# Where the query and key projections of a hybrid attention layer run: as jobs between attention steps, or as a stage of their own ahead of the linear attention

## The chip, the cores and the metric

The kernel runs on one core of a Trainium2 chip. The core has a matrix engine (TensorE, "PE" in the profile, its weight loads "PEld"), a vector engine (DVE), an activation engine (ACT), GpSimd (POOL) and SyncE (SP), which here issues the DMAs. Each engine works through its own instructions in order. The metric is the device time of one execution in microseconds (us); fewer is better.

## The reference

One inference step of one layer, for a prompt of 1024 frames and a sample of 32 further frames (together T = 1056 columns), model width 1024, everything in float32:

```python
gq, gk, gv, la, gg, dq, dk, dv, dg, ma, mb = in_proj(rmsnorm(hp, pre_norm_g), w_in, gla_w_a2, gla_b_a)
dq, dk = rope(dq, pos), rope(dk, pos)          # the first 16 of each 64 channels are rotated
o_gla, s_p = gla_prompt(gq, gk, gv, la)        # gated linear attention, 4 heads, chunked
o_diff = diff_prompt(dq, dk, dv, lam)          # 8 heads; two softmax maps m = 0, 1 per head
...
# diff_attend, per head and block of 128 queries:
s = q @ k / 8, masked by chunks of 64;  p = softmax(s)
attn = p[m=0] - lam * p[m=1];  out = attn @ v
...
yg = rmsnorm(o_gla) * silu(gg);  yd = rmsnorm(o_diff) * 0.8 * silu(dg)
merged = sigmoid(ma) * (yg @ w_proj_gla) + sigmoid(mb) * (yd @ w_proj_diff)
y = x + rmsnorm(merged @ w_out)
```

The rotated keys of all heads (`newk`) and the values are outputs too. The sample frames run the same layer against a cache of 512 past keys and values.

## The kernel before, in words

Activations stand as `X`: channels on the 128 partitions, 8 tiles deep, T columns, each split into a high and a low float32r part. A projection of 128 output channels is a **job**: 3 stretches of 352 columns, 8 tiles deep, and 3 matmuls each (high by high, low weights, low activations; L458, L459, L460), so 72 matmuls. `wtile` loads a job's weights (one raw buffer, two buffers for each split part), ACT makes the high part (L426), POOL the low part (L428).

The stages, in order: normalisation and the value projections (to 222 us of the profile); the linear attention ("GLA", 4 heads); the differential attention ("diff", 8 heads, which is the subject here); the output projection of the GLA branch; that of the diff branch (L436 to L438); the last projection and the norm (L1174 to L1196).

Inside the GLA and the diff stage the order on PE is written by a small planner, the class `Order`. Threads yield steps, each with a cost, a list of events that must have happened (with a latency after each) and the PSUM banks that it takes. `run` looks through the threads in their order and takes the first whose step is ready by the planner's own clock; the latencies are the table `W`, in us. The attention thread stands first, the sample thread second and `fill`, which works through the list of jobs in steps of 6 matmuls, last. So a job's matmuls are placed where attention would not yet be ready. The order so found is the order in which PE executes; on the chip it waits for the real semaphores. PE instructions of a later stage may be placed among those of an earlier one, but each stage keeps its own order.

In a diff head (`diff_main`, `diff_scores`) there are 8 query blocks i of 128 queries. For block i and each map m: the scores (L878, L879, width w = 128(i+1)) go to one of two large PSUM banks, DVE masks and takes the maximum (L880, L882), ACT the exponential (L884), and DVE combines the two maps (L887 to L889). Then PE transposes the result in groups of up to 4 blocks into the one bank "t" (L926), ACT and DVE split it (L928, L929), and after each second block the product with the values follows (L939 to L941). The scores of block i+1 are issued ahead of the transposes of block i. The head's end is `diff_fin` (L852 to L861), after the first scores of the next head. The latencies that pace this are `sm`, `sm_w`, `sm_s` (scores to a free bank), `p`, `p_w` (scores to the combined map), `tr_t` (transposes to a free bank: 2.27) and `at` (2.45).

The jobs of the diff stage before are: for each head a query job and a key job (`rot_job`), a job `dgate_job` for the silu gate (it needs `diff_fin` of the head before, and `diff_fin` of its own head needs it), and 12 of the 16 `gate_job`s for the merge gates, which can stand anywhere; `GATES_GLA` and `GATES_DIFF` say how many go with which head. A `rot_job` evacuates PSUM to one tile `rr`, fetches the partner channels of the rotation by four small DMAs, multiplies on POOL (L793) and DVE (L795), adds (L797), and splits into high and low parts (`split_q` L807 to L811, `split_k` L826 to L829, with DMAs that copy the halves of `k` and `kl` to the other 64 partitions). Queries have two buffers, keys one.

Of the kernel before, what the change touches and what calls it, by code (L numbers as in the profile page):

```python
# [11 lines left out]
F32 = mybir.dt.float32  # L12
# [31 lines left out]
GATES_GLA = [0, 1, 1, 1, 1]  # L44
GATES_DIFF = [2, 1, 1, 1, 1, 1, 1, 2, 2]
# [3 lines left out]
N = {"fin": 1, "rr": 3, "q": 2, "k": 4, "fill": 2, "first": 200, "evac": 1200, "lead": 2}  # L49
# [73 lines left out]
def hybrid_step_kernel(ctx: ExitStack, tc: tile.TileContext, a):  # L123
# [54 lines left out]
    ptd = dram.tile([KT, P, T], F32, name="ptd")  # L178

# [300 lines left out]

    gp = pool("gp", reuse_waits="tile")
# [273 lines left out]
    ct = dp.tile([P, T], F32, name="ct")  # L755
    dma(ct, a["ropec"])
    stb = dp.tile([P, T], F32, name="stb")
    dma(stb, a["ropes"])
    sw = dp.tile([P, T], F32, name="sw")
    nc.gpsimd.memset(sw, 0.0)  # L760

    for n, dt, tags in ((T, F32, ("rr",)), (NP, F32R, ("q00", "q10")), (NP, F32, ("p0", "p0", "p1")),
                        (NP, F32R, ("vh", "vl")), (NQ * 256, F32R, ("ah", "al")),
                        (NP, F32R, ("k0", "k1", "kl0", "kl1", "q01", "q11"))):
        for tag in tags:
            dp.tile([P, n], dt, tag=tag, bufs=tags.count(tag), name="first")
# [15 lines left out]
    SC = HD ** -0.5  # L782

    def rot_job(b, event, needs, split):
        def begin():
            r = dp.tile([P, T], F32, tag="rr", name="rr")

            def done():
                for m in range(2):
                    o = m * HD  # L790
                    dma(sw[o : o + 8], r[o + 8 : o + 16])
                    dma(sw[o + 8 : o + 16], r[o : o + 8])
                nc.gpsimd.tensor_tensor(sw, sw, stb, op=ALU.mult)  # L793
                for c in parts(T, N["rr"]):
                    ve.tensor_tensor(r[:, c], r[:, c], ct[:, c], op=ALU.mult)  # L795
                for c in parts(T, N["rr"]):
                    ve.tensor_tensor(r[:, c], r[:, c], sw[:, c], op=ALU.add)  # L797
                split(r)
            return (lambda ps, sl: act(r[:, sl], ps, AF.Copy)), done
        return b, event, begin, needs  # L800

    def split_q(h):
        def f(r):
            q0 = dp.tile([P, NP], F32R, tag=f"q0{h % 2}", name="q0")
            q1 = dp.tile([P, NP], F32R, tag=f"q1{h % 2}", name="q1")
            for c in parts(NP, N["q"]):
                act(q0[0:64, c], r[0:64, c], AF.Copy, scale=SC)  # L807
                act(q1[64:128, c], r[64:128, c], AF.Copy, scale=SC)
                ve.scalar_tensor_tensor(q0[64:128, c], r[0:64, c], SC, q0[0:64, c].bitcast(F32),
                                        op0=ALU.mult, op1=ALU.subtract)  # L810
                ve.scalar_tensor_tensor(q1[0:64, c], r[64:128, c], SC, q1[64:128, c].bitcast(F32),  # L811
                                        op0=ALU.mult, op1=ALU.subtract)
            qsam[h] = sam(0, h)
            act(qsam[h], r[:, NP:T], AF.Copy, scale=SC)
            dqs[h] = q0, q1
        return f

    def split_k(h):
        def f(r):
            st(a["newk"][h], r)  # L820
# [10 lines left out]
            for t, src, dst in ((k0, 0, 64), (k1, 64, 0), (kl0, 0, 64), (kl1, 64, 0)):  # L831
                dma(t[dst : dst + 64].bitcast(F32), t[src : src + 64].bitcast(F32))
# [449 lines left out]
```

## Time and profile before

| | |
|---|---|
| median of 3 runs | 1516.63 us (1512.86 to 1523.22) |
| the profiled execution | 1523.35 us, span 1521.6 us |
| granted PE clock, mean | 0.981 |
| PE busy | 1438.6 us, 95% of the span |
| PEld busy | 1340.6 us, 88% |
| DVE busy | 792.0 us, 52% |
| ACT busy | 623.2 us, 41% |
| POOL busy | 298.4 us, 20% |
| DMA queue of SP | 150.71 MB, 30.9% of 16 engines' span |

A row of a group reads: line, engine, operation, output <- inputs, shapes, count | busy us, mean ns of one | idle time ahead and what ended it. Matmuls overlap in the records: one of 352 columns is recorded with some 320 ns and the next starts 160 ns later, so for PE the distance of starts is the cost. A row of stretches reads: from:to, length, then busy us and count for each engine, the granted PE clock, the DMA share and GB/s.

### The profile page before, as it was taken

What the parts mean: (1) busy time and instruction counts of PE and PEld (TensorE: products, weight loads), DVE (VectorE), ACT (ScalarE), POOL (GpSimd) and SP (SyncE); (2) the same over time, 40 slices, a digit from 0 to 9 for tenths busy, and PEclk for the clock granted to TensorE, in tenths of its full rate; (3) what the DMA queues carried; (4) which work ended last, traced back from release to release, by engine and by line L of the source; (5) the groups of instructions that cost most, each with busy time, mean ns of one, the idle gap of its engine ahead of it and who ended that gap; (6) DMA issues with size and microseconds to landing.
All of it is one profiled execution on the core that took longest, in us unless ns stands there. A gap on an engine that the chain in (4) does not pass through costs nothing.

```text
span 1521.6 us, 22330 instructions
## 1 busy us (share of the span) xinstructions
PE 1438.6 (95%) x8848; PEld 1340.6 (88%) x8848; DVE 792.0 (52%) x1464; ACT 623.2 (41%) x1282; POOL 298.4 (20%) x186
## 2 busy tenths in 40 slices
PE   8999999989999998998999998989899999999997
PEld 6787789889989898998989897989798889999997
DVE  5602005655474343757685866677764544155415
ACT  4603114635353323564655564555555443022311
POOL 1200002222222233121222222212221112122001
PEclk9999999999999999999999998999999999999999
DMA  8621111221222144131323132223212187433305
GB/s 294 205 104 37 44 48 43 61 85 56 89 70 78 58 145 130 46 88 60 102 75 88 60 102 76 74 73 88 89 50 89 67 271 248 168 130 117 109 1 187
DMA packets 66118, 152.29 MB, mean 100 GB/s; under 512 B 9920, under 2 KB 28480, under 8 KB 65488
## 3 DMA queue, kind: packets, MB, share of 16 engines
q1 hardware_dynamic: 66000, 150.71, 30.9%
q8 instruction: 74, 1.21, 0.3%
q14 instruction: 44, 0.36, 0.1%
HBM read 100.16 MB, written 39.98 MB: 92 GB/s over the span
## 4 chain that ended last, share of the span: by engine, by line
PE 51%; DVE 7%; ACT 4%; DMA 2%; issue 1%; POOL 1%; SPq 0%; DVEq 0%; POOLq 0%; ACTq 0%
PE ps_w L458 9%; PE ps_w L459 9%; PE ps_w L460 9%; PE ps_w L437 2%; PE ps_w L436 2%; PE ps_w L438 2%; PE ps_c L1176 2%; PE ps_c L1174 2%; PE ps_c L1175 2%; PE ps_t L926 2%; PE ps_s L879 2%; PE ps_s L878 2%; DVE p L888 1%; DMA kl<-kl 1%; PE po L940 1%
## 5 line engine op out<-in xcount | busy, mean ns | idle before, releaser
L458 PE MATMUL ps_w<-X,wh 128*128 128x352 f32 x1344 | 455.2, 339 | 7.5 <-ACT k L489 3.2
L459 PE MATMUL ps_w<-X,wl 128*128 128x352 f32 x1344 | 440.2, 328 | 0.0
L460 PE MATMUL ps_w<-X,wh 128*128 128x352 f32 x1344 | 438.3, 326 | 0.0
L428 POOL TENSOR_TENSOR wl<-wr,wh 128x1024 fp32r<-128x1024 f32 x72 | 178.5, 2479 | 688.5 <-ACT wh L426 551.2
L458 PEld LDWEIGHTS ps_w<-X,wh 128*128 128x128 f32 x1344 | 257.9, 192 | 12.5 <-DVE sg L471 4.0
L459 PEld LDWEIGHTS ps_w<-X,wl 128*128 128x128 f32 x1344 | 257.9, 192 | 1.2 <-issue 1.2
L460 PEld LDWEIGHTS ps_w<-X,wh 128*128 128x128 f32 x1344 | 258.5, 192 | 0.0
L884 ACT ACTIVATE p<-ps_s,nm 128x256 f32<-128x256 f32 (+7 forms) x128 | 94.4, 740 | 60.8 <-DVE nm L882 35.9
L426 ACT ACTIVATE wh<-wr 128x1024 fp32r<-128x1024 f32 x72 | 75.9, 1054 | 61.0 <-PE ps_w L460 35.7
L283 PE MATMUL ps_v<-wh,X 128*128 128x512 f32 x248 | 97.6, 394 | 1.4 <-DVE X L222 1.4
L282 PE MATMUL ps_v<-wh,X 128*128 128x512 f32 x248 | 98.3, 397 | 0.0
L284 PE MATMUL ps_v<-wl,X 128*128 128x512 f32 x248 | 98.2, 396 | 0.0
L882 DVE TENSOR_REDUCE nm<-ps_s 128x1 f32<-128x256 f32 (+7 forms) x128 | 95.0, 746 | 2.7
L880 DVE MEMSET ps_s<- 64x64 f32 x128 | 14.3, 112 | 118.4 <-PE ps_s L879 116.9
L269 DVE TENSOR_TENSOR vo<-ps_v,vo 32x512 f32<-32x512 f32 x4 | 2.7, 679 | 140.7 <-ACT vo L268 140.7
L926 PE MATMUL ps_t<-ident,p 128*128 128x128 f32 x288 | 49.0, 280 | 25.6 <-DVE ps_s L880 13.8
L928 ACT ACTIVATE ah<-ps_t 128x512 fp32r<-128x512 f32 (+2 forms) x96 | 46.8, 488 | 58.5 <-PE ps_t L926 57.8
L878 PE MATMUL ps_s<-k,q 128*128 128x512 f32 (+2 forms) x192 | 69.3, 368 | 1.2 <-DMA k<-k 1.2
L879 PE MATMUL ps_s<-kl,q 128*128 128x512 f32 (+2 forms) x192 | 65.0, 354 | 4.0 <-DMA kl<-kl 3.8
L643 POOL TENSOR_TENSOR vl<-vr,vh 128x512 fp32r<-128x512 f32 (+1 forms) x20 | 24.8, 1238 | 223.2 <-ACT vh L642 223.2
L265 ACT ACTIVATE vo<-ps_v 128x512 f32<-128x512 f32 x32 | 19.0, 595 | 114.9 <-PE ps_v L284 114.5
L926 PEld LDWEIGHTS ps_t<-ident,p 128*128 128x128 f32 x288 | 35.9, 143 | 32.8 <-issue 22.5
(318 smaller groups left out, 3039.3 us busy)
## 6 DMA issues: line engine op xcount, KB each, us to landing
wr<-w SPq DMA_DIRECT2D x72, 512.0 KB
thd<-gate SPq DMA_DIRECT2D x16, 528.0 KB
xn<-xn SPq DMA_DIRECT2D x16, 512.0 KB
wr<-wv SPq DMA_DIRECT2D x16, 512.0 KB
newk<-rr SPq DMA_DIRECT2D x8, 528.0 KB
ygr<-ygd SPq DMA_DIRECT2D x8, 528.0 KB
tha<-thd SPq DMA_DIRECT2D x8, 528.0 KB
ydr<-ydd SPq DMA_DIRECT2D x8, 528.0 KB
```

The lines of the kernel that those rows point to most:

```text
L282: mm(ps, xk[:, 0, t0 : t0 + P], wh[:, k, :], start=(k == 0), stop=False)
L283: mm(ps, xk[:, 1, t0 : t0 + P], wh[:, k, :], start=False, stop=False)
L284: mm(ps, xk[:, 0, t0 : t0 + P], wl[:, k, :], start=False, stop=(k == KT - 1))
L428: nc.gpsimd.tensor_tensor(wl, wr, wh.bitcast(F32), op=ALU.subtract)
L458: mm(ps[:, :n], wh[:, k, :], src[k][:, 0, t0 : t0 + n], start=(k == 0), stop=False)
L459: mm(ps[:, :n], wl[:, k, :], src[k][:, 0, t0 : t0 + n], start=False, stop=False)
L460: mm(ps[:, :n], wh[:, k, :], src[k][:, 1, t0 : t0 + n], start=False, stop=(k == KT - 1))
L878: mm(ps[:, n0 : n0 + n], qs[m][:, qsl], ks[m][:, n0 : n0 + n], start=True, stop=False)
L879: mm(ps[:, n0 : n0 + n], qs[m][:, qsl], kls[m][:, n0 : n0 + n], start=False, stop=True)
L882: ve.tensor_reduce(nm, ps[:, 0:w], axis=AX.X, op=ALU.max, negate=True)
L884: act(p[:, 0:w], ps[:, 0:w], AF.Exp, bias=nm, accum_out=sm[:, m : m + 1])
L926: nc.tensor.transpose(ps[:, (j - j0) * P : (j - j0 + 1) * P], p[:, j * P : j * P + P], ident)
```

## The change

All 16 query and key projections move out of the diff stage into a stage between the value projections and the GLA stage. They are plain `proj` calls in an order of the scheduler's making, not jobs of the planner. Their results go to DRAM (`qd`, `kd`: 16 half heads of 64 channels by T). After each four heads of keys or of queries, `turn` loads the rotated channels of those four heads into one tile of 128 partitions, its partner channels into another, rotates once and stores them back. In the diff stage `head_load` loads a head's keys and queries from DRAM to both halves of the partitions and splits them; it stands at block 2 of the head before. Keys and queries have two buffers each. The planner's jobs are now 8 + 8 + 2 in the GLA stage (before: 8 + 8 + 4) and 8 + 14 in the diff stage (before: 16 + 8 + 12). The latencies `sm`, `p`, `tr_t`, `at` are as they were.

```diff
-GATES_GLA = [0, 1, 1, 1, 1]
-GATES_DIFF = [2, 1, 1, 1, 1, 1, 1, 2, 2]
+GATES_GLA = [0, 0, 1, 1, 0]
+GATES_DIFF = [2, 2, 2, 2, 2, 1, 1, 1, 1]
-N = {... "q": 2, "k": 4, ...}
+N = {... "q": 2, "k": 2, ...}
-W = {... "dq": 7.76, "dk": 14.32, ...}
+W = {... "dq": 16.0, "dk": 16.0, ...}
...
+    rq = pool("rq", reuse_waits="tile")
+    ct = rq.tile([P, T], F32, name="ct")
+    stb = rq.tile([P, T], F32, name="stb")
...
+    def turn(d, g, new):
+        part = lambda s: d[g * 8 : g * 8 + 8, s * 8 : s * 8 + 8, :]
+        r = rq.tile([P, T], F32, tag="r", name="r")
+        sw = rq.tile([P, T], F32, tag="sw", name="sw")
+        for s in range(2):
+            dma(r[s * HD : s * HD + HD], part(s))
+            dma(sw[s * HD : s * HD + HD], part(1 - s))
+        nc.gpsimd.tensor_tensor(sw, sw, stb, op=ALU.mult)
+        ve.tensor_tensor(r, r, ct, op=ALU.mult)
+        ve.tensor_tensor(r, r, sw, op=ALU.add)
+        for s in range(2):
+            st(part(s), r[s * HD : s * HD + HD])
+            if new is not None:
+                for h in range(4):
+                    o = r[s * HD + h * 16 : s * HD + h * 16 + 16]
+                    st(new[4 * g + h].rearrange("(m d) t -> m d t", m=2)[:, s * 8 : s * 8 + 8, :], o)
+
+    def qk_block(b, d, h, scale, new):
+        r = rq.tile([P, T], F32, tag="nat", bufs=3, name="nat")
+        proj(wtile(b + h), xs, lambda ps, sl: act(r[:, sl], ps, AF.Copy, scale=scale))
+        st(d[2 * h : 2 * h + 2], r)
+        if new is not None:
+            for m in range(2):
+                st(new[h, m * HD + 16 : m * HD + HD, :], r[m * HD + 16 : m * HD + HD])
+
+    for g in range(2):
+        for b, d, scale, new in ((BLK_DK, kd, 1.0, a["newk"]), (BLK_DQ, qd, SC, None)):
+            for h in range(4 * g, 4 * g + 4):
+                qk_block(b, d, h, scale, new)
+            turn(d, g, new)
+    rq.release()
...
-    def rot_job(...), split_q(h), split_k(h)
+    def head_load(h):
+        both = lambda d, m: d[2 * h + m, :, 0:NP].unsqueeze(0).to_broadcast([2, HD, NP])
+        ks, kls, qs = [], [], []
+        for m in range(2):
+            kh = dp.tile([P, NP], F32R, tag=f"k{m}", bufs=2, name=f"k{m}")
+            kl = dp.tile([P, NP], F32R, tag=f"kl{m}", bufs=2, name=f"kl{m}")
+            dma(kl.bitcast(F32), both(kd, m))
+            for c in parts(NP, N["k"]):
+                act(kh[:, c], kl[:, c].bitcast(F32), AF.Copy)
+                ve.tensor_tensor(kl[:, c], kl[:, c].bitcast(F32), kh[:, c].bitcast(F32), op=ALU.subtract)
+            ...
+        for m in range(2):
+            raw = tp.tile([P, NP], F32, tag="sg1", name="qraw")
+            dma(raw, both(qd, m))
+            q = dp.tile([P, NP], F32R, tag=f"q{m}", bufs=2, name=f"q{m}")
+            for c in parts(NP, N["q"]):
+                act(q[:, c], raw[:, c], AF.Copy)
+                ve.tensor_tensor(q[64:128, c], raw[64:128, c], q[64:128, c].bitcast(F32), op=ALU.subtract)
+            qs.append(q)
+        ... # the sample's 32 columns by two small DMAs
+        S.mark(("dq", h))
+        S.mark(("dk", h))
...
         for i in range(NQ):                       # diff_main
+                if i == 2 and h + 1 < DH:
+                    head_load(h + 1)
...
     for h in range(-1, DH):                       # the diff stage's jobs
         n = GATES_DIFF[h + 1]
-            jobs.append(rot_job(BLK_DQ + h + 1, ...))
         jobs += [gate_job(*gates.pop(0)) for _ in range(min(n, 1))]
-            jobs.append(rot_job(BLK_DK + h + 1, ...))
         if h >= 0:
             jobs.append(dgate_job(h))
         jobs += [gate_job(*gates.pop(0)) for _ in range(n - 1)]
+    head_load(0)
```

The matmuls of the kernel are the same in number and shape before and after.

More of the change, by code (lines that the diff above doesn't have):

```diff
@@ L178, in hybrid_step_kernel @@
     ptd = dram.tile([KT, P, T], F32, name="ptd")
+    qd = dram.tile([2 * DH, HD, T], F32, name="qd")
+    kd = dram.tile([2 * DH, HD, T], F32, name="kd")
     def x_pair(name):
@@ L781, in parts @@
         return [slice(i * n // cnt, (i + 1) * n // cnt) for i in range(cnt)]
[L782 to L800, printed above, removed]
```

60 lines of the change are left out of this document (13 added, 47 removed), and 2 rows, old and new, of the table W.

## The prediction

> **What bounds the kernel now.** First the page's busy times and its groups.
>
> ```profile
> PE 1438.6 (95%) x8848; PEld 1340.6 (88%) x8848; DVE 792.0 (52%) x1464; ACT 623.2 (41%) x1282; POOL 298.4 (20%) x186
> L458 PE MATMUL ps_w<-X,wh 128*128 128x352 f32 x1344 | 455.2, 339 | 7.5 <-ACT k L489 3.2 <-DVE sg L471 3.0 <-PEq L572 1.0
> ```
>
> PE is busy nearly all the time, and a job holds 24 of the L458 matmuls, so 1344 are 56 jobs. The change keeps every matmul, so the time can only move by what PE waits. To see where jobs stand I took the busy times by stretch, of L458 alone: the end of the GLA stage, three diff heads (first scores to first scores of the next) and the whole diff stage; then the same stages with all engines, and the projection of the diff branch, which runs as plain `proj` calls.
>
> ```profile
> 558.90:601.79 42.89, 27.71 (x86) 16.13 (x86) 1.00 0.43 129
> 601.79:674.53 72.74, 34.00 (x100) 19.38 (x100) 0.98 0.27 77
> 826.43:901.06 74.63, 32.52 (x96) 18.09 (x96) 1.00 0.29 85
> 1144.22:1220.70 76.48, 29.37 (x84) 16.35 (x84) 0.98 0.24 86
> 601.79:1220.70 618.91, 263.04 (x760) 147.56 (x760) 0.97 0.27 80
> ...
> 601.79:1220.70 618.91, 580.21 (x3628) 546.20 (x3628) 411.67 (x791) 325.97 (x717) 139.54 (x66) 0.97 0.27 80
> 1323.30:1415.50 92.20, 92.20 (x576) 92.20 (x576) 46.88 (x70) 19.19 (x31) 18.42 (x14) 1.00 0.37 123
> ```
>
> The last row gives a job's price: 8 jobs in 92.2 us without a gap, **11.53 us each**. The diff stage takes 618.9 us for 760 / 24 = 31.7 jobs (365 us), so 254 us, 32 us per head, are attention and waits. A head swallows 100, 96 or 84 of L458: 4.2, 4 or 3.5 jobs.
>
> The question that decides is whether the jobs pace a head, or the head's own chain. Head 7 answers: nothing after it needs a query or key job, its jobs ran out before its end, and it still took 76.5 us. So a head is paced by the planner's latencies and the jobs fill them. The same end of a head, transposes of block 7 up to the product with the values, is in the trace once with jobs in between (head 0) and once after the jobs had run out (head 7):
>
> ```profile
> 665.07 0.60 PE L926 MATMUL ps_t<-ident,p 128*128 128x128 f32 x4
> 668.39 0.60 PE L926 MATMUL ps_t<-ident,p 128*128 128x128 f32 x4
> 671.73 0.28 PE L939 MATMUL po<-ah,vh 128*128 128x256 f32 x1
> ...
> 1211.52 0.66 PE L926 MATMUL ps_t<-ident,p 128*128 128x128 f32 x4
> 1213.59 0.66 PE L926 MATMUL ps_t<-ident,p 128*128 128x128 f32 x4 [1.41 <-DVE al L929]
> 1215.92 0.39 PE L939 MATMUL po<-ah,vh 128*128 128x256 f32 x1 [0.36 <-ACT os__13011 L1015]
> ...
> 1218.92 0.27 PE L1024 MATMUL ps_so<-ident,os__13011 64*128 64x64 f32 x1
> ```
>
> Filled, the steps lie 3.32 and 3.34 us apart; bare, 2.07 and 2.33, with PE idle for 1.41; the product's 24 matmuls then take 3.0. A latency without jobs does not vanish: it shrinks to some two thirds, and what is left is PE standing still.
>
> **The change part by part.** *The new stage* has 16 jobs: 16 x 11.53 = **+184.4 us** if it is as dense as the quoted stage of `proj` calls. ACT evacuates as there; `turn`'s work lies beside PE. I add 2 us for its ends (bounds 0 and 40, rival 3). The GLA stage's first head must then wait for the memory of `ct` and `stb`:
>
> ```profile
> 600.54 4.77 DMA kl<-kl
> L793 POOL TENSOR_TENSOR sw<-sw,stb 128x1056 f32<-128x1056 f32 x16 | 40.9, 2554 | 16.2 <-DMA sw<-rr 13.0 <-DVE sg L471 1.9 <-DVE sm L887 1.3
> L795 DVE TENSOR_TENSOR rr<-rr,ct 128x352 f32<-128x352 f32 x42 | 22.0, 543 | 0.0
> L797 DVE TENSOR_TENSOR rr<-rr,sw 128x352 f32<-128x352 f32 x42 | 20.6, 510 | 0.0
> L829 DVE TENSOR_TENSOR kl<-rr,k 64x256 fp32r<-64x256 f32 x28 | 14.0, 501 | 0.8
> L811 DVE SCALAR_TENSOR_TENSOR q<-rr,q 64x512 fp32r<-64x512 f32 x14 | 13.4, 957 | 0.4
> L809 DVE SCALAR_TENSOR_TENSOR q<-rr,q 64x512 fp32r<-64x512 f32 x14 | 13.2, 941 | 1.2 <-ACT q L807 0.8
> L828 DVE TENSOR_TENSOR kl<-rr,k 64x256 fp32r<-64x256 f32 x28 | 11.6, 413 | 0.4
> L1155 DVE TENSOR_TENSOR C<-cwr,C 128x512 fp32r<-128x512 f32 x12 | 7.7, 685 | 6.4 <-ACT C L1154 6.4
> ```
>
> A store, a load (each at most the 4.77 of the DMA row) and POOL's 2.55: some 10 us after the last projection, of which the first two jobs of the stage (23 us) hide all but the planner's early gate steps: I take +4 (0 to 10).
>
> *The GLA stage* gives two gates to the diff stage. The last one counts there. The one after the keys of head 1 filled latencies of head 0; by the two-thirds above its 11.5 us save 6, not 11.5 (0 to 11.5). With the +4 the stage's end moves by **-2**.
>
> *The wait for head 0.* Before, 42.9 us lie between the GLA's last transposes and the first scores, filled by 86 / 24 = 3.6 jobs, two of them the query and key job. Now the loads need only memory; the two query halves pass one after the other through the tile that held the GLA's last gate: twice a DMA (4.77) and a split (three operations, estimated by the 0.685 of the DVE row for a tile of that size), about 13.7 us, with gate jobs beside it. **-30 us** (-43 if the loads come free at once, -20 if they queue on SP behind stores).
>
> *What leaves a head.* The quoted DVE rows L795 to L828 sum to 94.8 us in the diff stage, 12 per head; `head_load` brings 4 x 0.685 for the keys and at most as much for the queries, 5.5 per head. Keys are now loaded a head ahead, so the waits for their copies go:
>
> ```profile
> PE ps_t L926 <- DVE ps_s L880: 13.8, 9, 2.8
> PE ps_t L926 <- DVE sm L887: 5.3, 1, 5.3
> ...
> PE ps_s L879 <- DMA kl<-kl: 3.8, 4, 2.2
> ```
>
> That is 3.8 us in all for the copies, and of the 19 us behind a busy DVE a part. A fully filled head so goes from 77.4 us (618.9 / 8) to about 73.6, between head 0 (72.7) and head 3 (74.6). What is late next is the softmax chain itself, which the change leaves alone. `head_load`'s DMAs wait on SP for the one query tile; behind them stand weights, gate stores and the value load. The weights are a job ahead (11.5 us), so I cost that at nothing; without that cover it is some 5 us per head.
>
> *What is missing in a head.* Fillers: 22 jobs instead of 35.3 (31.7 + 3.6). The job list with the rule that the silu gate of head h waits for the end of head h-1 lets them run so: 1.5 ahead of head 0; 4.2 in head 0; 3.3 in head 1; 3, 3 in heads 2 and 3; 2, 2, 2 in heads 4 to 6; 1 in head 7. The planner is greedy, so the early blocks are filled and the late ones, the longest, stand bare. Head 3, its first stretch up to the scores of block 1, then the whole cut at the scores of blocks 4 and 6 and the transposes of block 7, shows how many of its 96 fall where:
>
> ```profile
> 826.43:832.79 6.36, 3.04 (x8) 1.50 (x8) 1.00 0.42 134
> ...
> 826.43:854.04 27.61, 13.00 (x38) 7.14 (x38) 1.00 0.26 80
> 854.04:868.64 14.60, 6.11 (x18) 3.42 (x18) 1.00 0.22 74
> 868.64:890.14 21.50, 10.00 (x30) 5.65 (x30) 1.00 0.13 31
> 890.14:901.06 10.92, 3.41 (x10) 1.88 (x10) 1.00 0.80 216
> ...
> 879.74 0.44 PE L878 MATMUL ps_s<-k,q 128*128 128x512 f32 x1
> ...
> 881.41 0.39 PE L879 MATMUL ps_s<-kl,q 128*128 128x512 f32 x1
> ...
> 887.50 1.27 DVE L889 SCALAR_TENSOR_TENSOR p<-p,sm 128x1024 f32<-128x1024 f32 x1
> ```
>
> The first 8 fall before the next silu gate is free, so two jobs (48) last to the scores of block 6, three (72) almost to the transposes of block 7, one (24) about to the scores of block 4. Bare, the last piece shrinks by (3.32 + 3.34) - (2.07 + 2.33) = 2.3 us. The third: scores of block 6 (7/8 of those of block 7), transposes and product of block 5 (4.4, and 18 matmuls, 2.2), scores of block 7 (879.7 to 881.8, 2.1 with the first transposes' start), its softmax from 881.8 to 888.8 (7.0): some 17.2 instead of 21.5, so 4.5. The second by the same steps (1.3, 2.3, 1.5, 1.5, 2.1 and 2 for the softmax of block 3) some 10.6 instead of 14.6, so 4. DVE allows no more: it is busy 411.7 / 8 = 51 us per head now and 45 after. Against the filled 73.6: heads 0 and 1 take 72.7 and 72; heads 2 and 3, 70.5 each; heads 4 to 6, 66.8 each; head 7, 62.8. Sum 549; with 5 for the clock (below) 554 instead of 618.9: **-65 us**, for 13.3 jobs (153 us) that left. Bounds: -24 (bare stretches do not shrink) and -181 (rival 1).
>
> *The clock after a wait.* The longest frequent wait and what follows it, and the bare end of head 7:
>
> ```profile
> 1156.70:1160.50 3.80, 1.01 (x7) 0.72 (x6) 3.73 (x5) 0.30 (x1) 2.50 (x1) 1.00 0.61 242
> 1160.50:1165.00 4.50, 4.50 (x20) 4.50 (x20) 2.71 (x7) 1.97 (x6) 0.00 (x0) 0.62 0.49 152
> 1209.00:1221.00 12.00, 8.72 (x63) 6.86 (x61) 3.17 (x9) 6.00 (x14) 2.89 (x2) 1.00 0.59 226
> ```
>
> After 2.8 us idle the granted clock was 0.62 for 4.5 us, 1.7 us lost; through waits of 1.4 us it stayed at 1.00. The bare heads have one long wait each, for the softmax of block 7, and only some will fall so: 5 us. The Trainium skill, "TensorE: Matmul & The Clock Gate", section "Part 1: The HAM clock gate", says that an idle window of about 3.4 us halves the array's clock until it was busy as long again; it speaks against the change. Here a shorter wait sufficed. By the page alone every bare stretch with such a wait would run at half rate, which is rival 4.
>
> **Sum**, against the profiled 1523.35 us: +184.4 + 2 - 2 - 30 - 65 = +89, so 1612. That execution lies 6.7 above the median of 1516.6; against the median the forecast is **1606 us**. With all terms at their ends at once (new stage 184 to 194, GLA -11.5 to +10, start -43 to -20, heads -100 to -45) it would be 1547 or 1656.
>
> **The rivals.** *1, not slower: the bare latencies close up.* If the padding in the planner's latencies is most of them, bare heads fall to the longer of PE's own work (24 us of attention: head 3's 74.6 less 96 x 3 x 0.16 of jobs and less 4.8 idle, the stage's 618.9 - 580.2 over 8; plus its jobs) and DVE's 45: 72.7, 62.5, 58.6 twice, 47 three times, 45, together 438, so -181; with -45 for the start and +184 the time is 1475. It decides below a mean of 58 us per head, where the heads' saving equals the 154 that the other terms cost. For it: DVE is busy only 66% of the stage. Against it: the bare end of head 7, and the 7.0 us softmax. 0.13.
>
> *2, bare stretches don't shrink,* because DVE and the head's loads collide there: heads 74.6, saving 24: 1647. Against it the bare steps of head 7. 0.08.
>
> *3, the new stage is not dense.* `turn`'s loads wait on SP for the stores of the head just projected, and the next job's weights stand behind them; four turns of up to 10 us: 1644. For it: one SP queue issues everything. Against it: the weights' slack of a job. 0.08.
>
> *4, half clock through the bare stretches:* their PE work by the pieces (22 + 7 + 6 us less jobs) is some 70 us over six heads, of which 55 would show in place of the 5: 1656. 0.09.
>
> *The change doesn't do what it says* if the scheduler leaves projections over for later gaps; I see no place for it, since they are ready first. The forecast keeps 0.62.
>
> The range 1550 to 1655 takes in rivals 2 and 3. The three runs of before span 0.7%, so 1% is about what can be told from no change. Faster by over 1%: 0.07; within: 0.06 (both rival 1); slower: 0.87.
>
> **What would show it.** The new stage: 384 of L436's kind in some 186 us at clock 1.00. In the diff stage: heads 0 and 1 near 73 us, heads 4 to 6 near 67 with 48 of L458 each, waits of PE for `al` and for the combined map in the late blocks, the waits for `kl` gone, and PE idle well over 100 us. Heads 4 to 7 near 50 us, or jobs still standing in their last blocks, would make it wrong.

## The result: 1918.7 us, 26% slower, and the profile after

The changed kernel takes 1918.71 us (median of 4 runs, 1915.42 to 1927.16) against 1518.49 us for the kernel before on the same chip (4 runs, 1512.86 to 1523.22). The ratio is 1.2646, with a 95% interval of 1.2584 to 1.2708. The forecast, 1606 us, had the sign right and the size far off. The range up to 1655 does not hold the time.

The page's busy times, its slices of TensorE and the clock, and its chain, each now for the changed kernel:

```profile
PE 1513.6 (79%) x8848; PEld 1394.9 (73%) x8848; DVE 719.3 (38%) x1344; ACT 610.1 (32%) x1234; POOL 262.9 (14%) x173
PE   8999998986879899516758593957384777999998
PEclk9999998987979999858879696968686887999999
PE 30%; DMA 20%; DVE 5%; ACT 4%; POOL 1%; issue 1%; SPq 0%; DVEq 0%; POOLq 0%; ACTq 0%
```

PE executes the same 8848 matmuls, but is busy for 79% of the span instead of 95%, and its holes lie in slices 17 to 34, the start and the whole of the differential attention. The fourth row says what fills them: a fifth of the chain that ended last is DMA (2% before); the page puts 11% of the span on `qraw<-qd` and 7% on `kl<-kd`, the loads in `head_load`.

The span by stage: the busy times by stretch for the changed kernel (new stage, GLA to its last transposes, wait for the first scores, diff stage), then the last three of these of the kernel before. The columns are those of the prediction's rows: length, PE, PEld, DVE, ACT, POOL, clock, DMA share, GB/s.

```profile
219.90:427.70 207.80, 191.61 (x1155) 189.80 (x1155) 14.74 (x7) 37.07 (x63) 43.16 (x18) 0.95 0.42 128
427.70:794.60 366.90, 306.72 (x1894) 292.15 (x1894) 180.62 (x306) 139.00 (x276) 84.63 (x52) 0.92 0.22 67
794.60:833.10 38.50, 7.95 (x49) 7.66 (x48) 5.32 (x9) 5.90 (x10) 2.35 (x1) 0.63 0.22 82
833.10:1608.50 775.40, 504.89 (x2830) 452.55 (x2830) 336.32 (x677) 287.19 (x629) 76.11 (x41) 0.80 0.17 58
```

```profile
222.30:558.90 336.60, 314.47 (x2036) 300.69 (x2036) 181.71 (x305) 142.49 (x283) 85.78 (x53) 0.99 0.23 73
558.90:601.79 42.89, 41.68 (x262) 41.42 (x260) 16.70 (x25) 15.94 (x30) 16.38 (x7) 1.00 0.43 129
601.79:1219.00 617.21, 580.02 (x3628) 546.14 (x3628) 411.25 (x788) 324.30 (x713) 139.54 (x66) 0.97 0.26 79
```

| stage, us | before | forecast | after | after, loads by rows (first experiment) |
|---|---|---|---|---|
| new stage | - | 186.4 | 207.8 | 207.7 |
| GLA | 336.6 | 334.6 | 366.9 | 368.1 |
| wait for the first scores | 42.9 | 12.9 | 38.5 | 11.0 |
| diff stage | 617.2 | 552.2 | 775.4 | 564.9 |
| rest | 302.6 | 302.6 | 305.2 | 306.0 |

So of the 303 us between the forecast's span (1521.6 + 89) and the measured 1913.7, 223 are in the diff stage, 26 in its start, and 53 in the two stages before it (21 and 32). The diff stage does 798 matmuls less than before and takes 158 us longer.

Who waits there is told by the list of waits, of which these are a part (who waited for what: total us, times, longest):

```profile
ACT q L838 <- DMA qraw<-qd: 148.9, 16, 11.9
DVE q L839 <- ACT q L838: 140.8, 19, 12.8
ACT k L829 <- DMA kl<-kd: 139.2, 16, 11.5
DVE kl L830 <- ACT k L829: 124.4, 16, 9.6
PE ps_t L938 <- DVE al L941: 57.5, 18, 9.7
PE ps_s L888 <- ACT p L894: 53.4, 6, 9.9
PE ps_s L888 <- DVE q L839: 52.5, 2, 30.6
```

Read it from the top. All 32 loads (16 for keys, 16 for queries) are waited for, some 9 us each, 288 us in total; ACT stands in front of its split, and DVE in front of its own behind that. Both engines work in order, so the softmax steps queued behind the split (`p`, L894) and the transposed maps (`al`, L941) come up to 10 us late. The last row is of the first scores of head 0, which wait for their queries twice, 30.6 and 21.9 us. PE's own list names DVE and ACT, and no load. A reader who looks at PE alone sees a slow softmax; the DMA is two steps back.

What a load is like is seen in the timelines of SP and ACT for one pair of key loads (a row reads: start, length, engine, line, operation, output <- input, count, and in brackets the idle time ahead and what ended it), and in the busy times by stretch: a store of 528 KB (901 to 903), the first key load (929 to 939), the second (939 to 949).

```profile
926.81 1.41 SPq L827 DMA_DIRECT2D kl<-kd  x2
939.46 0.63 ACT L829 ACTIVATE k<-kl 128x512 fp32r<-128x512 f32 x1 [8.50 <-DMA kl<-kd]
949.61 1.15 ACT L829 ACTIVATE k<-kl 128x512 fp32r<-128x512 f32 x2 [8.27 <-DMA kl<-kd]
...
901.00:903.00 2.00, 2.00 (x16) 1.87 (x15) 1.35 (x4) 0.69 (x2) 1.57 (x1) 1.00 0.66 270
929.00:939.00 10.00, 6.18 (x40) 5.88 (x38) 2.18 (x4) 1.96 (x4) 0.00 (x0) 0.97 0.14 54
939.00:949.00 10.00, 6.80 (x28) 6.16 (x28) 2.95 (x4) 1.88 (x4) 0.00 (x0) 0.69 0.13 52
```

Both loads are issued at 926.8 and land one after the other, ten microseconds apart, at 52 to 54 GB/s. The DMA share is the key: 0.13 to 0.14 of 16 engines is **two engines**. It could also be sixteen engines that each move now and then, but the trace's record of single packets rules that out: in these two stretches exactly two packets are in flight for 82% and 96% of the time, and hardly ever fewer. The store at 901 has 0.66 and 270 GB/s. Each load writes 512 KB to 128 partitions from 64 rows, with the two copies (`unsqueeze(0).to_broadcast([2, HD, NP])`) as the outermost dimension.

That is the theory to be tested: a DMA whose outermost dimension is 2 runs on two engines. The Trainium skill, "DMA: Bandwidth & Descriptors", section "Why a DMA increments its semaphore by 16 and not by 1", states that the number of engines is the largest one up to 16 that divides the outermost dimensions which are not 1; its rules for kernel authors name a leading broadcast. By that rule these loads get two engines, and the trace agrees with 0.13 of 16. The rival: the loads are late because SP issues them late, or because any four loads in a row overrun their time.

### The profile page after: what moved, and what is told of

It is laid out like the page before. It is cut to its first block, busy times and chain, and to the rows that moved or that the text cites. A ratio compares the mean times of both kernels' runs of the same rounds, so it can differ in the third digit from the quotient of the medians.

```text
span 1913.7 us, 22128 instructions
## 1 busy us (share of the span) xinstructions
PE 1513.6 (79%) x8848; PEld 1394.9 (73%) x8848; DVE 719.3 (38%) x1344; ACT 610.1 (32%) x1234; POOL 262.9 (14%) x173
## 4 chain that ended last, share of the span: by engine, by line
PE 30%; DMA 20%; DVE 5%; ACT 4%; POOL 1%; issue 1%; SPq 0%; DVEq 0%; POOLq 0%; ACTq 0%
DMA qraw<-qd 11%; DMA kl<-kd 7%; PE ps_w L461 4%; PE ps_w L462 4%; PE ps_w L463 4%; PE ps_t L938 2%; PE ps_w L440 2%; PE ps_w L439 2%; PE ps_w L441 2%; PE ps_c L1184 2%; PE ps_c L1182 2%; PE ps_c L1183 2%; PE ps_s L888 1%; PE ps_s L889 1%; PE po L952 1%; PE po L951 1%
## 5 line engine op out<-in xcount | busy, mean ns | idle before, releaser
L461 PE MATMUL ps_w<-X,wh 128*128 128x352 f32 x960 | 334.0, 348 | 13.1 <-ACT gate L480 5.3
L462 PE MATMUL ps_w<-X,wl 128*128 128x352 f32 x960 | 323.1, 337 | 0.0
L463 PE MATMUL ps_w<-X,wh 128*128 128x352 f32 x960 | 321.2, 335 | 0.0
L431 POOL TENSOR_TENSOR wl<-wr,wh 128x1024 fp32r<-128x1024 f32 x72 | 174.3, 2420 | 914.5 <-ACT wh L429 773.9
L461 PEld LDWEIGHTS ps_w<-X,wh 128*128 128x128 f32 x960 | 193.2, 201 | 16.2 <-ACT gate L480 5.6
L462 PEld LDWEIGHTS ps_w<-X,wl 128*128 128x128 f32 x960 | 191.9, 200 | 0.3 <-issue 0.2
L463 PEld LDWEIGHTS ps_w<-X,wh 128*128 128x128 f32 x960 | 191.7, 200 | 0.0
L888 PE MATMUL ps_s<-k,q 128*128 128x512 f32 (+2 forms) x192 | 73.8, 391 | 106.0 <-ACT p L894 53.4
L938 PE MATMUL ps_t<-ident,p 128*128 128x128 f32 x288 | 58.2, 319 | 105.2 <-DVE al L941 57.5
L439 PE MATMUL ps_w<-X,wh 128*128 128x352 f32 x384 | 125.9, 329 | 13.3 <-ACT wh L429 12.6
L440 PE MATMUL ps_w<-X,wl 128*128 128x352 f32 x384 | 126.7, 330 | 2.9 <-POOL wl L431 2.9
L441 PE MATMUL ps_w<-X,wh 128*128 128x352 f32 x384 | 125.2, 326 | 0.0
L888 PEld LDWEIGHTS ps_s<-k,q 128*128 128x128 f32 x192 | 39.3, 205 | 114.1 <-ACT p L894 55.2
L894 ACT ACTIVATE p<-ps_s,nm 128x256 f32<-128x256 f32 (+7 forms) x128 | 94.1, 740 | 50.0 <-DVE ps_s L890 38.9
L429 ACT ACTIVATE wh<-wr 128x1024 fp32r<-128x1024 f32 x72 | 76.0, 1055 | 96.9 <-DMA wr<-w 39.7
L439 PEld LDWEIGHTS ps_w<-X,wh 128*128 128x128 f32 x384 | 73.8, 193 | 14.2 <-ACT wh L429 13.2
L501 DVE TENSOR_TENSOR r<-r,ct 128x1056 f32<-128x1056 f32 x4 | 5.0, 1259 | 198.0 <-DMA r<-kd 97.4
```

What stands on the lines that cost most here:

```text
L431: nc.gpsimd.tensor_tensor(wl, wr, wh.bitcast(F32), op=ALU.subtract)
L439: mm(ps[:, :n], wh[:, k, :], src[k][:, 0, t0 : t0 + n], start=(k == 0), stop=False)
L440: mm(ps[:, :n], wl[:, k, :], src[k][:, 0, t0 : t0 + n], start=False, stop=False)
L441: mm(ps[:, :n], wh[:, k, :], src[k][:, 1, t0 : t0 + n], start=False, stop=(k == KT - 1))
L461: mm(ps[:, :n], wh[:, k, :], src[k][:, 0, t0 : t0 + n], start=(k == 0), stop=False)
L462: mm(ps[:, :n], wl[:, k, :], src[k][:, 0, t0 : t0 + n], start=False, stop=False)
```

## Experiments

All ratios are to the kernel before, on the same chip, with three rounds each. The kernel of the first experiment, the *rows-outer kernel*, is the base of the later ones unless something else is said.

**1. The loads by rows.** Each broadcast load becomes two loads of 64 rows, so that rows are outermost. Bytes, tiles, splits and order stay.

```diff
-            dma(kl.bitcast(F32), both(kd, m))
+            for s in range(2):
+                dma(kl.bitcast(F32)[s * HD : s * HD + HD], kd[2 * h + m, :, 0:NP])
... # the queries in the same way
```

> The changed kernel with each load of head_load written as two DMAs of 64 rows instead of one whose outermost dimension is a broadcast of 2. Theory (transfers on 2 of 16 DMA engines): in the changed kernel ACT waits 139 us for kl and 149 us for qraw, about 9 us for each of 32 loads, and DVE, PE behind it; with all engines a load takes 2 to 3 us, these waits fall under 60 us in all, a head takes some 68 us as forecast, and the time is 1600 to 1660. Rival (the split's place in the queues of ACT and DVE, whatever the transfer): the waits stay, over 1800. Rival (the shortage of filler jobs is far dearer than forecast): waits for DMA fall but PE's idle in the heads stays, over 1750.

Measured: 1677.0 us, ratio 1.1038 (1.0995 to 1.1081): **242 us less** than the changed kernel, and 17 above the theory's range. The waits on the same loads, and the wait for the first scores and the diff stage by stretch:

```profile
ACT q L840 <- DMA qraw<-qd: 12.1, 9, 3.5
ACT k L831 <- DMA kl<-kd: 2.0, 3, 0.7
...
798.10:809.10 11.00, 8.77 (x49) 8.48 (x47) 5.74 (x7) 4.64 (x8) 2.40 (x1) 0.90 0.87 213
809.10:1374.00 564.90, 480.41 (x2830) 433.16 (x2830) 338.64 (x679) 290.57 (x631) 76.53 (x41) 0.90 0.27 81
```

288 us of waiting became 14, and the first loads now move at a DMA share of 0.87. The diff stage fell by 210.5 us and its start by 27.5. What is left, 159 us over before, comes from elsewhere than the waits for these loads.

**2 and 3. One kind of load at a time.** In the rows-outer kernel either the queries' or the keys' loads are written with the broadcast again.

> The rows-outer kernel with only the two query loads of a head written with the broadcast of two outermost, as in the changed kernel; the keys' loads stay two loads of 64 rows. Theory (each such load runs on 2 of 16 DMA engines, about 10 us, and ScalarE and VectorE stand in line for it): queries and keys each carry about half of the 242 us, total 1677 + 100 to 150 = 1777 to 1827. Rival (only the four loads in series, 40 us a head, overrun what the planner has as lead; two fit into it): total within 30 us of 1677.

> The rows-outer kernel with only the two key loads of a head written with the broadcast of two outermost; the queries' loads stay two loads of 64 rows. The mirror of the queries' case, which cost 113 us of 242. Theory (each load holds its two DMA engines for about 10 us and ScalarE stands in line; the costs add): 1677 + 100 to 145 = 1777 to 1822. Rival (keys have two buffers, so their loads are issued a head ahead and are hidden where the queries' loads are not in the way): within 40 us of 1677.

Queries by two: 1790.4 us, ratio 1.1781 (1.1750 to 1.1812), +113. Keys by two: 1803.8 us, ratio 1.1871 (1.1837 to 1.1904), +127. The waits, first of the queries' kernel, then of the keys':

```profile
ACT q L840 <- DMA qraw<-qd: 149.2, 16, 11.8
ACT k L831 <- DMA kl<-kd: 2.3, 5, 0.7
```

```profile
ACT k L831 <- DMA kl<-kd: 141.3, 16, 11.1
ACT q L840 <- DMA qraw<-qd: 15.0, 10, 3.7
```

The two costs add to 240 of the 242. The rival that keys are covered by their two buffers falls, and so does the other one, that two slow loads would fit into the planner's lead where four do not. The likely reason, which no run tests by itself, is that the split stands in ACT's line soon behind the load's issue, whatever the number of buffers.

**4 to 6. Is it enough that something reads the load?** The waits say that a split waits for its own load. But two engines held for 10 us could also delay everybody else's data. To part the two, unread copies were added to the rows-outer kernel.

```diff
+        for n, d in enumerate((kd, qd)):
+            for m in range(2):
+                dma(junk[h, m, n], d[2 * h + m, :, 0:NP].unsqueeze(0).to_broadcast([2, HD, NP]))
```

> The rows-outer kernel with four further copies a head, of the same keys and queries with the broadcast of two outermost, into scratch in DRAM that nothing reads, issued behind head_load's own loads. Theory (the 242 us are the wait of ScalarE's and VectorE's splits for those very loads): the copies hold two DMA engines for about 40 us a head but nothing waits for them, total within 25 us of 1677. Rival (the two engines are held, and every other load's share on them comes late): total 100 us or more above 1677.

Measured: 1876.1 us, ratio 1.2372 (1.2327 to 1.2417), +199. Both theories had placed the copies in the diff stage, and this is not where they ran: their inputs are ready early, and they were issued from 303 us on. The diff stage took 574.4 us, against 564.9, and the cost fell on the new stage and on GLA. There SP's timeline shows another order than in the rows-outer kernel:

```profile
375.45 0.35 SPq L514 DMA_DIRECT2D kd<-nat  x1
375.85 1.24 SPq L517 DMA_DIRECT2D newk<-nat  x2
377.20 0.72 SPq L428 DMA_DIRECT2D wr<-w  x1
378.39 0.63 SPq L849 DMA_DIRECT2D jk<-qd  x1
401.02 0.35 SPq L514 DMA_DIRECT2D kd<-nat  x1
```

The next weights (`wr<-w`) are issued only behind the store of the projection just computed, so no job's weights are ahead and a projection takes 25 us instead of 12. The run says nothing on the question. The next one binds each copy to the diff stage by a store of 4 KB of the split keys into the same scratch:

```diff
+            for n, d in enumerate((kd, qd)):
+                dma(junk[h, m, n][0, 0:1, :], kl[0:1, :].bitcast(F32))
+                dma(junk[h, m, n], d[2 * h + m, :, 0:NP].unsqueeze(0).to_broadcast([2, HD, NP]))
```

> The rows-outer kernel with four further copies a head in the differential attention, of keys and queries with the broadcast of two outermost, into scratch that nothing reads; each is behind a 4 KB store of the split keys into the same scratch, so that it can't be issued ahead of that head's splits. Theory (the 242 us are ScalarE's and VectorE's wait in line for the loads they read): nothing reads the copies, so the stage from the first score to the last value product, 564.5 us in the rows-outer kernel, grows by under 30 us, and the total stays within 30 us of 1677; what it grows by is weights and values that arrive late, and would show as waits of ScalarE for wr and vr. Rival (two of the 16 DMA engines held for some 40 us a head delay every other load's share on them): the stage grows by 100 us or more.

Measured: 1919.9 us, ratio 1.2666 (1.2608 to 1.2725), **+243**, though nothing reads the copies. My theory that two held engines cost nobody but the reader of the load falls. One load of queries, by rows, shows what happens (timelines of SP and ACT, then three stretches):

```profile
990.24 1.15 SPq L825 DMA_DIRECT2D qraw<-qd  x2
1005.82 1.15 ACT L844 ACTIVATE q<-qraw 128x512 fp32r<-128x512 f32 x2 [23.68 <-DMA qraw<-qd]
...
973.00:990.00 17.00, 8.38 (x61) 8.06 (x60) 3.05 (x8) 2.90 (x8) 3.30 (x2) 0.88 0.13 51
991.00:994.00 3.00, 0.00 (x0) 0.00 (x0) 0.00 (x0) 0.00 (x0) 0.00 (x0) 0.50 0.73 205
994.00:1004.00 10.00, 0.00 (x0) 0.00 (x0) 0.00 (x0) 0.00 (x0) 0.00 (x0) 0.50 0.13 53
```

The copies hold two engines from 973 on. The load by rows is issued at 990.24; in three microseconds (share 0.73) most of it is through, and then for ten more microseconds only two engines move (0.13), while ACT waits and every other engine stands still. The load's parts on these two engines lie behind the copies. The Trainium skill, "DMA: Bandwidth & Descriptors", section "Queues, rings and completion order", says that each DMA engine takes its descriptors in ring order; the stretch agrees. A part of the cost is of this run's own making, though. Ahead of that load SP itself stands: its two instructions before it, a copy and a 4 KB store, last 7.4 and 9.8 us, and over the kernel it waits 97.3 us, eight times, until a 4 KB store has landed, before it issues the copy behind it. The last run of the three takes the two engines away: each copy is written as two of 64 rows, behind the same 4 KB stores.

```diff
-                dma(junk[h, m, n], d[2 * h + m, :, 0:NP].unsqueeze(0).to_broadcast([2, HD, NP]))
+                for s in range(2):
+                    dma(junk[h, m, n][s], d[2 * h + m, :, 0:NP])
```

> The kernel with four further unread copies a head (1919.9 us), the same bytes into the same scratch behind the same 4 KB stores, but each copy as two of 64 rows without the broadcast. Theory (two of the 16 DMA engines held by the outermost broadcast are what costs): the bytes and the order on SP's queue stay, the engines are shared, and the total falls back to within 40 us of the rows-outer kernel's 1677 (up to 1717). Rival (the 4 KB stores and further 64 issues in SP's order cost the 243 us, whatever engines the copies use): total 1850 or more. Between the two: both count, by the share.

Measured: 1688.2 us, ratio 1.1099 (1.1061 to 1.1136), +11. The edit does not keep quite all the rest: of the 64 half copies 32, it seems those that the 4 KB store does not overlap, were issued between 301 and 470 us, ahead of the diff stage. The other 32 stand in it, as many as in the run before with half its bytes, and the stage took 567.7 us against 772.1. SP's wait for the 4 KB stores is down from 97.3 us to 1.3. So bytes, stores and issues cost 11 us in all, and the 232 us between the two runs are what the two engines cost, in late shares and in an SP that stands; how they divide, and what the other half of the bytes would add in the stage, these runs do not show. In the changed kernel itself what lies behind a slow load is mostly the next slow load and its split: ACT's wait for weights over the whole kernel is 39.7 us there and 39.8 with loads by rows, the same. SP waits for a query load 84.4 us ahead of the next one and 46.3 us ahead of the value load.

**7 and 8. What a job in the diff stage is worth.** The forecast's model of a head was that latencies pace it, jobs fill them, and bare stretches shrink. One kernel adds 13 gate jobs (150 us of PE work into scratch) to the diff stage, the other moves 14 of the gates there ahead, into the new stage.

```diff
-GATES_DIFF = [2, 2, 2, 2, 2, 1, 1, 1, 1]
+GATES_DIFF = [3, 3, 3, 3, 3, 3, 3, 3, 3]    # 13 further jobs
... # or, in the other kernel:
+GATES_DIFF = [0] * 9                        # 14 gates as plain projections in the new stage
```

> e1 with 13 further jobs in the diff stage (gate projections computed a second time into a scratch tensor), so that there are 35 as before: 150 us of PE work more. Theory (bare latencies): the jobs go into waits, heads take 73 to 76 us, and the time is 55 to 80 us above e1. Rival (PE is the bound in e1's heads too, or they wait for something else): 140 to 155 us above e1.

> e1 with the 14 merge gates of the diff stage computed in the dense stage ahead, so that a diff head has only its silu gate as a job: the same PE work, 161 us of it moved out of the heads. Theory (bare latencies): a head keeps about 60 us, so the heads lose some 60 to 80 us and the time is 80 to 100 us above e1. Rival (PE is the bound): within 15 us of e1.

13 more jobs: 1756.2 us, ratio 1.1567 (1.1528 to 1.1606), +79 for 150 us of work. 14 jobs moved ahead: 1794.1 us, ratio 1.1813 (1.1773 to 1.1853), +117. The diff stage in the two:

```profile
809.10:1436.40 627.30, 580.20 (x3641) 548.46 (x3642) 353.80 (x675) 319.56 (x677) 104.05 (x51) 0.95 0.30 92
```

```profile
975.00:1498.50 523.50, 380.91 (x1852) 312.88 (x1852) 323.86 (x672) 258.24 (x572) 42.21 (x26) 0.76 0.21 57
```

From the barest to the fullest the stage takes 523.5, 564.9 and 627.3 us. Fourteen jobs, 161 us of work, cost it 41; the next thirteen, 62 (the rest of their 79 lies behind the stage). So a job costs a quarter to two fifths of its length there in these two runs, and whoever takes jobs out gets only a part of their length back (the eleventh and twelfth run, with two jobs less, gave two fifths to a half). The clock follows the filling: 0.76, 0.90, 0.95. The first kernel's heads took 78.4 us in the mean, above the 73 to 76 expected. The second kernel came out above its theory: bare heads (65 us) shrink less than I expected.

**9 to 12. The 21 and 32 us of the two earlier stages.** In the new stage PE waits twice for weights; the first list is of the rows-outer kernel in that stage, with the first gate step of GLA behind it:

```profile
PE ps_w L439 <- ACT wh L429: 12.4, 2, 6.4
PE ps_w L440 <- POOL wl L431: 2.9, 2, 1.5
...
PE ps_z L552 <- DVE t L554: 12.6, 1, 12.6
```

```profile
393.69 0.61 SPq L504 DMA_DIRECT2D kd<-r  x1
394.34 3.50 SPq L508 DMA_DIRECT2D newk<-r  x4
397.89 0.62 SPq L504 DMA_DIRECT2D kd<-r  x1
398.55 2.65 SPq L508 DMA_DIRECT2D newk<-r  x4
401.30 0.35 SPq L513 DMA_DIRECT2D qd<-nat  x1
402.51 0.34 SPq L427 DMA_DIRECT2D wr<-w  x1
```

The second fence is SP's timeline: behind `turn` of four key heads SP waits for the rotated tile and issues ten stores, eight of them small, ahead of the next weights. The first try left out the last `turn` (the queries of heads 4 to 7 are not rotated in it):

```diff
-            turn(d, g, new)
+            if new is not None or g == 0:
+                turn(d, g, new)
```

> e1 without the last call of turn, which leaves out the rotation of the queries of heads 4 to 7. Theory (the GLA stage's first head waits for that turn, whose loads wait for the last stores): 12 to 25 us below e1, and the 12.8 us wait of ps_z for DVE goes. Rival (hidden by the first jobs, as forecast): within 5 us of e1.

Measured: 1656.5 us, ratio 1.0929 (1.0878 to 1.0980), 20.5 less. GLA took 355.4 us instead of 368.1, which is 12.7 of it, and PE's 12.6 us wait for DVE in the first gate step is no longer in the list: that was DVE standing in order in the last `turn`, whose loads land late. The second try put `turn`'s arithmetic and stores two projections later in the program:

```diff
         for s in range(2):
             ... # loads of r and sw
+        return lambda: turn_rest(d, g, new, part, r, sw)   # multiplies, add, stores: called two blocks later
```

> The rows-outer kernel (1677.0 us, each of head_load's loads as two loads of 64 rows) with turn cut in two: its loads are still issued right behind the four projections, its multiplies, add and stores only after two further projections. Theory (SP's queue): in the rows-outer kernel the new stage takes 207.7 us, 21 over the forecast, because the store behind turn's add waits on SP ahead of the weights' next load; with the multiplies done later nothing on SP waits for them, PE's two stalls of about 6 us go, and the first head of the gated linear attention no longer finds VectorE held in turn. Stage 185 to 193 us, total 15 to 35 us less: 1642 to 1662. Rival (the stage is limited by the 16 eight-block jobs and their evictions whatever turn does): stage still 200 to 210 us, total within 5 us of 1677.

Measured: 1678.75 us, ratio 1.1033 (1.0978 to 1.1087), no change. The edit did not do what it says: SP issued `turn`'s stores and the weights in the same order, but for one projection's store that moved up, and within about a microsecond of the same times, and PE waited for the weights 12.5 us in two, as before the edit. The run tells nothing on its theory. Here, as with the first unread copies, an instruction's place in the program did not set its place in the queue. The third set two gates back into GLA:

```diff
-GATES_GLA = [0, 0, 1, 1, 0]
-GATES_DIFF = [2, 2, 2, 2, 2, 1, 1, 1, 1]
+GATES_GLA = [0, 1, 1, 1, 1]
+GATES_DIFF = [1, 2, 2, 2, 2, 1, 1, 1, 0]
```

> The rows-outer kernel with the gates' tables set back as far as the changed stages allow: four gate jobs in the gated linear attention (heads 1 to 4) instead of two, 14 instead of 16 in the differential attention. Theory (bare latencies pace the gated linear attention's heads too: its two remaining jobs' removal saved nothing, the heads' intervals are 74.0, 84.7, 84.2, 54.8 us against 69.5, 82.5, 82.3, 52.1 with four jobs): the two jobs, 23 us of TensorE work, cost that stage 0 to 8 us, and the differential attention gets 0 to 8 us shorter; total 1669 to 1685. Rival (a gate job costs its 11.5 us wherever it stands): the stage of the gated linear attention gets 23 us longer, the other 23 shorter; total the same but the stages' spans differ. Second rival (jobs are worth more to the heads than that, as moving 14 of them ahead cost 117 us): the total is 16 us or more above 1677.

Measured: 1659.9 us, ratio 1.0920 (1.0852 to 1.0988), 17 less, beyond the theory's range on the better side. GLA and the diff stage of that kernel, by stretch:

```profile
431.60:792.10 360.50, 321.22 (x2040) 306.71 (x2039) 180.30 (x307) 144.59 (x286) 89.85 (x54) 0.97 0.23 74
802.50:1355.90 553.40, 459.92 (x2686) 410.88 (x2686) 335.01 (x679) 286.48 (x623) 71.83 (x39) 0.89 0.27 79
```

With 23 us more work GLA is 7.6 us *shorter* than the 368.1 of the rows-outer kernel: its clock rises from 0.92 to 0.97, PE's busy time by only 12.7 us (308.5 in the rows-outer kernel), and its idle time falls by 20. The diff stage gains 11.5 from two jobs less. The last run adds to this kernel one store of a half's rotated keys in place of four:

```diff
-                for h in range(4):
-                    o = r[s * HD + h * 16 : s * HD + h * 16 + 16]
-                    st(new[4 * g + h].rearrange("(m d) t -> m d t", m=2)[:, s * 8 : s * 8 + 8, :], o)
+                st(new[4 * g : 4 * g + 4].rearrange("h (m d) t -> (h m) d t", m=2)[:, s * 8 : s * 8 + 8, :], r[s * HD : s * HD + HD])
```

> The gates-back kernel (four gate jobs in the gated linear attention, 1659.9 us, ratio 1.092 to before) with turn's eight small stores of rotated keys, four for each half, as one store for each half. Theory (SP's queue): behind turn's two keys' stores SP spends 3.5 and 2.7 to 4.0 us on the eight small ones before it issues the next weights, and TensorE stands 6.2 to 6.6 us for wh twice in the new stage. With two stores for eight SP is free some 5 us earlier each time: the two stalls shrink to 1 to 2 us, the stage by 8 to 11 us, the total by 6 to 12 us (1648 to 1654). Rival (the wait for turn's add ahead of these stores holds SP, not their number): stalls within 1 us of 6.3, total within 4 us of 1660.

Measured: 1650.75 us, ratio 1.0892 (1.0844 to 1.0939), 9 less; the intervals of the two totals overlap, so the stage is the better witness. The new stage:

```profile
221.70:417.10 195.40, 187.55 (x1154) 186.64 (x1153) 14.75 (x7) 36.52 (x63) 43.28 (x18) 0.99 0.44 136
PE ps_w L439 <- ACT nat L510: 7.8, 3, 3.7
```

The stage falls from 210.0 (in the kernel with gates back) to 195.4, its clock is 0.99, and the wait for weights is gone from PE's list. That SP's time for the eight stores is the whole reason is not shown by it, because a second thing changes with them: the destination of a small store has two groups of eight rows outermost (`m`, of size 2), that of the one store eight groups. In the rows-outer kernel the weights that SP issued at 402.51 are waited for until 413.04, and in two stretches of that time the DMA share is again that of two engines:

```profile
407.00:409.00 2.00, 1.14 (x8) 0.85 (x6) 0.00 (x0) 0.46 (x1) 0.00 (x0) 1.00 0.13 46
412.00:413.00 1.00, 0.00 (x0) 0.00 (x0) 0.00 (x0) 0.00 (x0) 0.00 (x0) 0.50 0.12 50
```

The single packets of the trace tell who moves: those of the stores have 4224 bytes, those of the weights 4096. The weights' packets go from 403.5 to 407, then there is none until 411, while the stores' packets go on two engines, and the last weights' packets follow from 411 to 412.5. So the mechanism of the first experiment delays these weights by some 4 us, on top of the time that SP takes to issue them; how the 14.6 us of the stage divide between the two, no run shows. This is the fastest form found of the changed structure, and it is still 8.9% slower than the kernel before. No version that I ran beats that one.

## Why the prediction was wrong in size

**The step that failed** is the price of `head_load`'s DMAs. The prediction took "twice a DMA (4.77)" for the start. For the other heads it gave the loads no term at all: "I cost that at nothing" is said of the weights, gate stores and value load that stand behind them on SP, with 5 us per head as the price without cover, and what ACT and DVE would wait for the loads themselves is not in the sum. The 4.77 us belonged to a copy of another form. A row can give the duration of a transfer of the same shape; this one's outermost dimension of two was a property that no row of before showed. Measured: some 10 us a load, four in a row per head, 288 us of waiting on ACT, 242 us of the kernel's time. The diff's line with `to_broadcast([2, HD, NP])` was there to be read, and the Trainium skill's rule quoted above would have made it a rival of its own. None of my rivals had this mechanism; rival 3 named SP's queue, not the DMA engines.

**The start of head 0**, -30, was missed with it (measured -4), and comes out at 42.9 to 11.0, -31.9, once the loads go by rows.

**The heads**, -65: with loads by rows -52.3 (617.2 to 564.9), a mean of 70.6 us per head against the forecast's 69.3 (554 / 8, with its clock term). The single heads take 77.0, 82.0, 65.7, 78.1, 63.8, 71.7, 62.7 and 63.8: the sum holds better than the pattern. Head 7, which loads nothing, took 64.5 us in the changed kernel too (forecast 62.8); it alone was right before any experiment. That the sum comes so near is in good part luck, for two errors cancel. The forecast let a filled head fall from 77.4 us to 73.6; with 13 jobs put back the stage took 627.3 us, 78.4 a head, so filled heads did not get shorter. The step was not covered by its lines either: 3.8 us a head is 30 in the stage, and the waits quoted beside it are 22.9 in all. Against that, taking the jobs away gave 62.4 us (627.3 to 564.9), where the forecast had 35 (eight times 73.6, to 554). Rival 1, bare latencies that close up to 55 us a head, falls: with 14 further jobs taken out the heads still took 65. Rival 2 falls as well.

**The clock**, +5, was too small. In the rows-outer kernel PE is busy 480.4 us for 2830 matmuls; the 580.0 us of before less 798 matmuls at 0.16 are 452, so the lower clock (0.90) costs 28 us of busy time. The heads' sum came out only 13 above the forecast all the same, so part of the 28 must lie where PE would else have waited; how much, no run shows. The trace's clock has two values only, full and half, so 0.90 is a fifth of the stage at half rate. The 28 us lie midway between the forecast's 5 and the 55 of rival 4, half rate through all bare stretches; neither is borne out. At 0.80 in the changed kernel it is more, but there the long waits of the loads come in.

**The new stage**, +184.4 +2: measured 207.8. The density was that of the row, but for two stalls (15 us with the waits for `wl`) and the clock after them. "`turn`'s work lies beside PE" held for DVE and POOL and not for SP's queue and the transfers. Rival 3 was near: it put the next weights behind `turn`'s loads on SP, and the runs show them late behind `turn`'s small stores, in SP's order and on the two engines that these stores hold. Its price, four times 10 us, was too high, since only the two `turn`s with the small stores stall PE.

**GLA**, -2: measured +30. The wait for `ct` and `stb` that I put at +4 is a wait for DVE, which is held in the last `turn`: leaving that out gave 12.7 us in GLA. The gate whose removal was to save 6 saved nothing; with two gates back GLA got 7.6 us shorter. That is 20 of the 32 us by which GLA with the loads by rows lies above before; for the other 11 I have no run, and their cause stays open. I had applied to GLA the two-thirds rule of a diff head without a row of GLA.

**The sum with the loads by rows** is 1677, 71 above the forecast: 21 from the new stage, 33 from GLA, 13 from the heads, and small terms.

## What to carry to other kernels

Before a transfer is priced by a row of the trace, look at its outermost dimension: 512 KB with two copies outermost took 10 us on two engines, and as two loads by rows it was all but hidden. A slow DMA is also paid by those who don't read it: a later transfer with a share on the same engines lands behind it, and an issuing queue that waits for one stands with all that follows. And jobs that fill another chain's latencies cost only a part of their length where they stand: taken out here, they gave back a quarter to a half of it, and the clock of what remained was lower.

## What was not expected of the hardware

Two engines are not just a slow transfer: a 16-engine load issued behind them had most of its bytes moved in 3 us and landed 10 us later. And the clock goes with how full PE is, not only with single long waits. In the diff stage of the kernel with the gates ahead it fell to half 28 times, and before 22 of these no wait of PE in the 6.8 us ahead was longer than 2 us. The mean granted clock of the diff stage was 0.97 before, 0.95 with 13 added jobs, 0.90 with loads by rows, 0.76 with the gates gone, and in GLA, with two more jobs, it was 0.97 in place of 0.92 and the stage was shorter.
